# Stick breaking: a part of the products of sigmoid and running product moved from VectorE to GpSimd

## The chip, the cores and the metric

The kernel runs on one core of a Trainium2 chip. The core has five engines that matter here: PE (TensorE), VectorE (DVE in the profile), ScalarE (ACT), GpSimd (POOL) and SyncE (SP), which issues the transfers. Each executes its own list of instructions in order and waits on semaphores for the others. The metric is the device time of one execution in microseconds; lower is better. Times before are three runs: 3091.64, 3101.06 and 3104.94 us, median 3101.06 us.

## The reference

Two encoder layers over 2064 tokens (16 meta tokens and 2048 others) of width 1024. The first has eight stick-breaking heads beside eight latent-attention heads (MLA), the second eight sliding-window heads (SWA) beside eight forgetting heads (FoX). The change touches only the stick breaking:

```python
z = jnp.einsum('bqhd,bkhd->bhqk', q[:, q0:q1], k[:, :q1]).astype(jnp.float32) * scale
past = jnp.arange(q1)[None, :] < jnp.arange(q0, q1)[:, None]
log_stay = jnp.where(past, jax.nn.log_sigmoid(-z), 0.0)
log_after = lax.cumsum(log_stay, axis=3, reverse=True) - log_stay
w = jnp.where(past, jnp.exp(jax.nn.log_sigmoid(z) + log_after), 0.0)
outs.append(jnp.einsum('bhqk,bkhd->bqhd', w.astype(v.dtype), v[:, :q1]))
```

The weight of a key is sigmoid(z) of that key, times the product of sigmoid(-z) over the keys between it and the query.

## The kernel before

The tokens are held in reverse order, so that the keys between a key and the query stand ahead of it in a row, and the sum over logarithms becomes a running product from left to right. A tile is 128 queries; its keys go in chunks of at most 512 columns (the last one with the 16 meta keys). For each pair of heads and each chunk, PE puts the scores of both heads into two PSUM banks (line 1087). For each head `sb_sig` then emits five steps:

1. ScalarE: sigmoid(-z) from the bank into columns 1 to n of `b` (`sig1`, line 1407). `b` and `pc` are the two halves of one row buffer of 1026 fp32; there are four such buffers (`sbr`).
2. VectorE: a scan forms the running product of `b` into `pc` (`scan`, line 1415 for the first chunk, 1417 for the others, which start from the last column of the chunk before).
3. ScalarE: sigmoid(z) in place in the PSUM bank (`sig2`, line 1410). It needs the scan for nothing.
4. VectorE: `pc` = bank times `pc` (line 1431), when both are there (`signed`). After it `mulled` gives the bank back and announces the chunk.
5. `pv_hi`: ScalarE casts `pc` to fp16 (line 1205, for meta keys 1207), then VectorE or GpSimd subtracts to form the low half (line 1218, for meta keys 1220). Then a DMA transposes both halves (line 588) and PE multiplies them with the values (lines 1278 to 1280).

While these go on, the same engines make the projections of the next heads: PE at lines 825 and 915, ScalarE and VectorE at lines 936, 937, 970, 972, 1770 and 1771, and the preparation of weights at lines 653, 655, 698 and 755 (VectorE, ScalarE, GpSimd).

The order on every engine comes from a planner, `Flow`, when the program is built. It keeps a clock of its own, a queue of jobs for each engine by priority, and for each engine a sum of the costs that stand in its queue or run, `f.load`. Costs are formulas, as `dve(n)` = 1.042 n + 69 ns and `gps(n)` = 1.88 n + 150 ns. A job is emitted when the planner's clock has its engine free. Of the subtraction of step 5 the planner decides where it goes by these loads, when the cast is done:

```python
onD = f.load["D"] + d + LOBIAS < f.load["G"] + g      # line 1213, LOBIAS = 1000 ns
```

So a job that is moved or costed otherwise changes the order of everything that follows, on all engines.

Of the kernel before, what the change touches and what calls it, by code (L numbers as in the profile page):

```python
# [15 lines left out]
AF = mybir.ActivationFunctionType  # L16
ALU = mybir.AluOpType
# [3 lines left out]
D = 1024  # L21
# [379 lines left out]
def act(n, ap=False, sb=False):  # L401
    return 0.834 * n + 50.0 + (93.0 if ap else 0.0) + (42.0 if sb else 0.0)


def dve(n):
    return 1.042 * n + 69.0


def gps(n):
    return 1.88 * n + 150.0  # L410
# [15 lines left out]
class Kern:  # L426
# [974 lines left out]
    def sb_sig(self, ps, n, e, i, prev, read, v):  # L1401
        nc, f, it = self.nc, self.f, e.it
        r, pr = it.r, it.pr
        b, pc = v[:, 0:513], v[:, 513:1026]

        def sig1():
            nc.scalar.activation(b[:r, 1:n + 1], ps[:r, :n], AF.Sigmoid, scale=pr.scn[:r])  # L1407

        def sig2():
            nc.scalar.activation(ps[:r, :n], ps[:r, :n], AF.Sigmoid, scale=pr.scp[:r])  # L1410

        def scan():
            if i == 0:

                nc.vector.tensor_tensor_scan(pc[:r, :n + 1], b[:r, :n + 1], self.diag[:r, :n + 1], 0.0, ALU.mult, ALU.add)
            else:
                nc.vector.tensor_tensor_scan(pc[:r, :n + 1], b[:r, :n + 1], self.diag[:r, :n + 1], prev[0], ALU.mult, ALU.bypass)  # L1417
            prev[0] = pc[:r, n:n + 1]

        both = [2]  # L1420

        def scanned():

            if i:
                read(i - 1)
            signed()

        def signed():
            both[0] -= 1
            if not both[0]:  # L1430
                f.job("D", dve(n), lambda: nc.vector.tensor_tensor(pc[:r, :n], ps[:r, :n], pc[:r, :n], ALU.mult), mulled, e.pr)  # L1431

        def mulled():
            self.bk.free("S", ps)
            e.done = lambda: read(i)
            self.pv_ready(e, pc)

        f.job("A", act(n, True), sig1, lambda: f.job("D", 2.08 * n + 135.0, scan, scanned, e.pr), e.pr)
        f.job("A", act(n, True), sig2, signed, e.pr)


    def sm_item(self, pr, u, mask, done, stored):
# [2022 lines left out]
```

## Time and profile before

| | |
|---|---|
| median of three runs | 3101.06 us |
| the profiled execution | 3114.27 us |
| its span in the trace | 3112.2 us |
| busy: PE, VectorE, ScalarE, GpSimd | 84%, 78%, 57%, 51% |
| stick breaking | about 100 to 1000 us |
| mean granted clock of PE | 0.94 of full speed |

An engine's busy time is the time in which it had an instruction running, and an instruction that waits inside itself, for a port for example, counts as busy. Idle time stands beside the next instruction, with what ended it. The stages of the kernel overlap: while stick breaking runs, PE already makes projections for what follows.

### The profile page before, as it was taken

The page shows a single profiled execution, that of the slowest core. Times are in us where ns is not written, and L with a number is a line of the kernel's source. Part 1 is how long each engine was busy: PE and PEld are TensorE (multiplying, and loading weights), DVE is VectorE, ACT ScalarE, POOL GpSimd, SP SyncE. Part 2 cuts the span into 40 slices and gives each one's busy share as a digit, 9 for nine tenths or more (in the row PEclk, how much of TensorE's full clock was granted, in tenths as well). Part 3 has the DMA queues.
Part 4 walks back from the last instruction along what each step waited for, and adds up shares of the span by engine and source line. Part 5 has one row for each costly group of instructions (what it writes and reads, how often), then busy time and mean ns, then how long its engine had stood idle before and what let it go on. Part 6 is the DMA issues. An engine that isn't in the chain of part 4 may idle for free. (4 is left out here: it accounts for less than half of the span.)

```text
span 3112.2 us, 88537 instructions
## 1 busy us (share of the span) xinstructions
PE 2608.2 (84%) x34261; PEld 1794.9 (58%) x34261; DVE 2439.8 (78%) x6874; ACT 1775.4 (57%) x4082; POOL 1576.6 (51%) x2292
## 2 busy tenths in 40 slices
PE   4888988888887798888776799968969797799998
PEld 2676766766775455545554355646746465566643
DVE  8889899989998786667686875866757576588866
ACT  4667677757875465556575335455465554566611
POOL 3566566755754354445465534344454443456500
PEclk9989999999998999999887899989989899899999
DMA  4365465666798699999999985777667666555863
GB/s 153 54 125 108 98 120 113 114 115 108 128 162 186 166 196 215 221 212 188 164 166 168 215 205 87 145 134 141 115 125 134 118 128 107 101 123 100 177 166 112
DMA packets 1206808, 444.62 MB, mean 143 GB/s; under 512 B 1091616, under 2 KB 1171584, under 8 KB 1206384
## 3 DMA queue, kind: packets, MB, share of 16 engines
q1 hardware_dynamic: 1204048, 430.50, 71.1%
q0 software_dynamic: 2336, 8.46, 0.8%
q8 instruction: 268, 4.39, 0.6%
q14 instruction: 156, 1.28, 0.1%
HBM read 119.62 MB, written 51.06 MB: 55 GB/s over the span
## 5 line engine op out<-in xcount | busy, mean ns | idle before, releaser
L1218 POOL TENSOR_TENSOR mem<-mem 128x512 f16<-128x512 f32 (+3 forms) x751 | 823.6, 1107 | 440.4 <-ACT mem L1205 414.1
L825 PE MATMUL bank<-mem 128*128 128x512 f16 (+2 forms) x4272 | 929.1, 369 | 8.7 <-DVE mem L1485 2.6
L1205 ACT CAST mem<-mem 128x512 f16<-128x512 f32 (+3 forms) x1080 | 520.3, 513 | 276.6 <-DMA mem<-mem 134.4
L825 PEld LDWEIGHTS <-mem 128*128 128x128 f16 (+1 forms) x4272 | 405.9, 100 | 438.6 <-issue 88.2
L1278 PE MATMUL psO<-mem 128*128 128x64 f16 x3264 | 403.8, 200 | 294.4 <-DMA mem<-mem 287.8
L915 PE MATMUL bank<-mem 128*128 128x128 f16 x9984 | 643.7, 221 | 5.5 <-DVE mem L970 4.1
L915 PEld LDWEIGHTS <-mem 128*128 128x128 f16 x9984 | 578.3, 99 | 49.4 <-issue 41.0
L1087 PE MATMUL bank<-mem 64*128 64x256 f16 (+8 forms) x6264 | 521.3, 286 | 47.4 <-DVE mem L1431 22.5
L1278 PEld LDWEIGHTS <-mem 128*128 128x128 f16 x3264 | 307.4, 101 | 426.9 <-DMA mem<-mem 367.0
L1522 ACT ACTIVATE mem<-mem,smt,p 128x656 f32<-128x656 f32 (+16 forms) x264 | 336.3, 1275 | 237.3 <-DVE smt L1519 206.7
L1280 PE MATMUL psO<-mem 128*128 128x64 f16 x3264 | 400.6, 199 | 0.0
L1279 PE MATMUL psO<-mem 128*128 128x64 f16 x3264 | 400.5, 199 | 0.0
L1087 PEld LDWEIGHTS <-mem 64*128 64x128 f16 (+1 forms) x6264 | 271.8, 96 | 195.8 <-issue 100.1
L1279 PEld LDWEIGHTS <-mem 128*128 128x128 f16 x3264 | 310.3, 102 | 15.2 <-issue 2.4
L1280 PEld LDWEIGHTS <-mem 128*128 128x128 f16 x3264 | 311.1, 102 | 0.0
L1218 DVE TENSOR_TENSOR mem<-mem 128x512 f16<-128x512 f32 (+3 forms) x329 | 254.8, 791 | 66.4 <-ACT mem L1205 62.9
L1417 DVE TENSOR_TENSOR_SCAN mem<-mem 128x513 f32<-128x513 f32 (+2 forms) x224 | 290.7, 1325 | 4.9 <-ACT mem L1407 4.6
L1550 POOL TENSOR_TENSOR ist<-ist,p 128x2 f32<-128x2 f32 (+1 forms) x196 | 49.7, 254 | 425.1 <-DVE ist L1547 406.1
L1490 DVE CUSTOM_DVE_ANT_0 mem<-bank,mem 128x256 f32<-128x256 f32 (+6 forms) x484 | 195.5, 455 | 74.2 <-PE bank L1093 48.9
L1407 ACT ACTIVATE mem<-bank,p 128x512 f32<-128x512 f32 (+3 forms) x360 | 213.1, 592 | 45.0 <-PE bank L1087 44.4
L1325 POOL TENSOR_TENSOR mem<-mem 128x128 f16<-128x128 f32 (+1 forms) x264 | 136.9, 522 | 176.1 <-ACT mem L1322 174.3
L1485 DVE TENSOR_SCALAR_CACHE_REDUCE mem<-bank 128x512 f32<-128x512 f32 (+5 forms) x372 | 188.8, 545 | 38.3 <-PE bank L1093 22.6
(191 smaller groups left out, 4130.2 us busy)
## 6 DMA issues: line engine op xcount, KB each, us to landing
mem<-in_w_dram SPq DMA_DIRECT2D x46, 512.0 KB, 4.0
tmp_mx_dram<-mem SPq DMA_DIRECT2D x128, 128.0 KB, 2.4
mem<-in_wout_dram SPq DMA_DIRECT2D x32, 512.0 KB, 4.3
mem<-mem SPq DMA_TRANSPOSE x988, 3.4
mem<-tmp_cqT_dram SPq DMA_DIRECT2D x12, 1024.0 KB, 6.5
mem<-in_xr_dram SPq DMA_DIRECT2D x16, 512.0 KB, 4.5
tmp_res_dram<-mem POOLq DMA_DIRECT2D x16, 512.0 KB, 5.0
mem<-tmp_res_dram SPq DMA_DIRECT2D x16, 512.0 KB, 5.3
```

Source lines behind the costliest of these rows:

```text
L825: nc.tensor.matmul(out, lhsT=st(kt, a), rhs=mv(kt, b), start=i == 0 and j == 0, stop=i == m - 1 and j == 2)
L915: nc.tensor.matmul(ps[:, 128 * i:128 * i + 128], lhsT=mv(a)[:, kt, 128 * i:128 * i + 128], rhs=w[b][:, kt, c0:c0 + 128], start=i == 0 and ...
L1087: nc.tensor.matmul(o, lhsT=l, rhs=m, start=i == 0, stop=mask is None and i == len(run) - 1)
L1205: nc.scalar.copy(t[:r, a:a + w], e.P[:r, e.pcol:e.pcol + w])
L1218: eng.tensor_tensor(t[:r, a + w:a + 2 * w], e.P[:r, e.pcol:e.pcol + w], t[:r, a:a + w], ALU.subtract)
L1278: nc.tensor.matmul(out, lhsT=p[:, a, :r], rhs=vt[:, hd, 0, :], start=e.first and i == 0 and hd == 0, stop=False)
L1279: nc.tensor.matmul(out, lhsT=p[:, a, :r], rhs=vt[:, hd, 1, :], start=False, stop=False)
L1280: nc.tensor.matmul(out, lhsT=p[:, b, :r], rhs=vt[:, hd, 0, :], start=False, stop=False)
L1407: nc.scalar.activation(b[:r, 1:n + 1], ps[:r, :n], AF.Sigmoid, scale=pr.scn[:r])
L1417: nc.vector.tensor_tensor_scan(pc[:r, :n + 1], b[:r, :n + 1], self.diag[:r, :n + 1], prev[0], ALU.mult, ALU.bypass)
L1490: nc.vector.tensor_tensor_reduce(row[:r, o + oo:o + oo + w], ps[:r, oo:oo + w], pr.cum[kb][hd][:r, ko:ko + w], 1.0, -3e38, ALU.add, ALU.ma ...
L1522: nc.scalar.activation(row[:r, :n], row[:r, :n], AF.Exp, bias=st[:r, 1:2], scale=sc[:r], accum_out=it.st[:r, hd:hd + 1])
```

## The change

When `sb_sig` is called for a chunk of a head, it compares two loads of the planner: `onG` holds if GpSimd's load with the new multiplication (1.15 times `gps(n)`) is less than VectorE's load. If it doesn't hold, the five steps are as before. If it holds:

- step 3 is emitted only after the scan (`sig3`, line 1428 of the changed kernel), and writes sigmoid(z) into columns 1 to n of `b`, in place of the sigmoid(-z) that the scan has read. At its end the PSUM bank is given back;
- step 4 is on GpSimd (`weigh`, line 1425): `pc` = `b` times `pc`, all in on-chip memory;
- step 5 follows as before.

```diff
         both = [2]
+        d, g = dve(n), 1.15 * gps(n)
+        onG = f.load["G"] + g < f.load["D"]
+
+        def weigh():
+            nc.gpsimd.tensor_tensor(pc[:r, :n], b[:r, 1:n + 1], pc[:r, :n], ALU.mult)
+
+        def sig3():
+            nc.scalar.activation(b[:r, 1:n + 1], ps[:r, :n], AF.Sigmoid, scale=pr.scp[:r])
 
         def scanned():
 
             if i:
                 read(i - 1)
-            signed()
+            if onG:
+                f.job("A", act(n, True), sig3, lambda: [self.bk.free("S", ps), f.job("G", g, weigh, mulled, e.pr)], e.pr)
+            else:
+                signed()
...
         def mulled():
-            self.bk.free("S", ps)
+            if not onG:
+                self.bk.free("S", ps)
             e.done = lambda: read(i)
             self.pv_ready(e, pc)
 
         f.job("A", act(n, True), sig1, lambda: f.job("D", 2.08 * n + 135.0, scan, scanned, e.pr), e.pr)
-        f.job("A", act(n, True), sig2, signed, e.pr)
+        if not onG:
+            f.job("A", act(n, True), sig2, signed, e.pr)
```

Lines behind the change move: the multiplication that stays on VectorE is line 1442 of the changed kernel, and all lines from 1442 of before on stand 13 lower.

How this looks in the lists of instructions, at its first place, two scans of 273 columns early in the stick breaking. VectorE, the difference (- before, + changed); `mem` is on-chip memory, `bank` a PSUM bank, `p` a column of scale factors:

```order
 L1417 SCALAR_TENSOR_TENSOR mem<-mem 128x273 x2
-L1431 TENSOR_TENSOR mem<-bank_85,mem 128x272
-L1431 TENSOR_TENSOR mem<-bank_84,mem 128x272
 L98 TENSOR_SCALAR p2t<-p_24_376 128x1
 L110 TENSOR_SCALAR p_32_801<-p2t 128x1
```

The two multiplications behind the scans are gone from VectorE; the next work follows the scans at once.

ScalarE at the same place, the difference:

```order
 L1407 ACTIVATE mem<-bank_85,p_24_376 128x272
-L1410 ACTIVATE bank_85<-bank_85,p_24_376 128x272
 L1407 ACTIVATE mem<-bank_84,p_24_376 128x272
-L1205 CAST mem<-mem 128x256
-L1410 ACTIVATE bank_84<-bank_84,p_24_376 128x272
-L1205 CAST mem<-mem 128x256
+L1205 CAST mem<-mem 128x256 x2
+L1407 ACTIVATE mem<-bank_83,p_24_376 128x512
+L1428 ACTIVATE mem<-bank_85,p_24_376 128x272
+L1428 ACTIVATE mem<-bank_84,p_24_376 128x272
```

The second sigmoid no longer follows the first of its bank; both stand behind two casts and the first sigmoid of the next chunk, and write on-chip memory instead of the bank.

GpSimd at the same place, before:

```order
L790 TENSOR_TENSOR nr<-amr,half 128x1 x3
L1218 TENSOR_TENSOR mem<-mem 128x256 x3
L1220 TENSOR_TENSOR mem<-mem 128x2x16
L1218 TENSOR_TENSOR mem<-mem 128x256
L1220 TENSOR_TENSOR mem<-mem 128x2x16
L1218 TENSOR_TENSOR mem<-mem 128x512 x2
```

and in the changed kernel:

```order
L790 TENSOR_TENSOR nr<-amr,half 128x1 x3
L1218 TENSOR_TENSOR mem<-mem 128x256 x2
L1425 TENSOR_TENSOR mem<-mem 128x272 x2
L1218 TENSOR_TENSOR mem<-mem 128x256
L1220 TENSOR_TENSOR mem<-mem 128x2x16
L1218 TENSOR_TENSOR mem<-mem 128x256
L1220 TENSOR_TENSOR mem<-mem 128x2x16
L1218 TENSOR_TENSOR mem<-mem 128x512 x2
```

The two multiplications stand ahead of the subtractions of their own chunk, and all that follows on GpSimd stands behind them. Counted over the whole lists: 119 multiplications are on GpSimd and 241 stay on VectorE; 26 subtractions of line 1218 and 9 of line 1220 go from GpSimd to VectorE.

## Rows read from the trace of the kernel before

**Rows 1.** Page, heading and busy time of the engines over the span.
```profile
span 3112.2 us, 88537 instructions
PE 2608.2 (84%) x34261; PEld 1794.9 (58%) x34261; DVE 2439.8 (78%) x6874; ACT 1775.4 (57%) x4082; POOL 1576.6 (51%) x2292
```
**Rows 2.** Busy us, 100 to 1000: PE, PEld, DVE, ACT, POOL; clock, DMA, GB/s.
```profile
100.00:1000.00 900.00, 769.34 (x11737) 596.30 (x11736) 841.82 (x1405) 641.69 (x1467) 569.60 (x571) 0.97 0.65 121
```
**Rows 3.** Line 1417: count, duration min/median/max in ns, first and last start.
```profile
L1417 DVE TENSOR_TENSOR_SCAN mem<-mem x224: 487/1274/2460, 118.6 to 990.5; 128x513 f32<-128x513 f32 x48, 128x273 f32<-128x273 f32 x28, 128x145 f32<-128x145 f32 x12, 128x401 f32<-128x401 f32 x12
```
**Rows 4.** Waits, 100 to 1000 us, by engine: waiter, releaser, us, times, longest.
```profile
DVE mem L1364 <- PE psO L1282: 10.0, 13, 1.9
DVE mem L1417 <- ACT mem L1407: 4.6, 4, 1.6
...
ACT mem L1205 <- DVE mem L1431: 54.7, 53, 3.4
...
POOL mem L1218 <- ACT mem L1205: 229.3, 140, 4.9
...
PE psO L1278 <- DMA mem<-mem: 72.6, 74, 4.2
```
**Rows 5.** Timeline of VectorE and GpSimd, 439 to 456 us: start, us, what.
```profile
439.39 1.21 DVE L1415 TENSOR_TENSOR_SCAN mem<-mem 128x513 f32<-128x513 f32 x1
439.65 1.66 POOL L1218 TENSOR_TENSOR mem<-mem 128x384 f16<-128x384 f32 x1 [3.09 <-ACT mem L1205]
441.47 0.92 POOL L1218 TENSOR_TENSOR mem<-mem 128x384 f16<-128x384 f32 x1
...
447.05 1.28 DVE L1417 TENSOR_TENSOR_SCAN mem<-mem 128x513 f32<-128x513 f32 x1 [1.58 <-ACT mem L1407]
...
450.83 1.16 POOL L1218 TENSOR_TENSOR mem<-mem 128x512 f16<-128x512 f32 x1 [4.58 <-ACT mem L1205]
451.19 0.67 DVE L1431 TENSOR_TENSOR mem<-bank,mem 128x512 f32<-128x512 f32 x1
...
452.47 0.75 DVE L1417 TENSOR_TENSOR_SCAN mem<-mem 128x257 f32<-128x257 f32 x1
...
454.14 2.87 POOL L755 TENSOR_TENSOR mem<-mem 128x1024 bf16<-128x1024 f16 x1
455.18 2.38 DVE L1417 TENSOR_TENSOR_SCAN mem<-mem 128x257 f32<-128x257 f32 x1
```
**Rows 6.** Instructions by line and shape, 100 to 1000 us: busy us, mean ns, idle.
```profile
L1417 DVE TENSOR_TENSOR_SCAN mem<-mem 128x513 f32<-128x513 f32 x96 | 157.9, 1667 | 3.6 <-ACT mem L1407 3.3
L1431 DVE TENSOR_TENSOR mem<-bank,mem 128x512 f32<-128x512 f32 x192 | 123.8, 674 | 0.8
L1431 DVE TENSOR_TENSOR mem<-bank,mem 128x144 f32<-128x144 f32 x32 | 8.3, 290 | 0.0
L1218 DVE TENSOR_TENSOR mem<-mem 128x512 f16<-128x512 f32 x6 | 4.8, 796 | 0.0
L1407 ACT ACTIVATE mem<-bank,p 128x512 f32<-128x512 f32 x192 | 132.8, 691 | 28.0 <-PE bank L1087 27.6
L1218 POOL TENSOR_TENSOR mem<-mem 128x512 f16<-128x512 f32 x186 | 273.3, 1483 | 158.6 <-ACT mem L1205 140.9 <-issue 12.9 <-DMA mem<-in_ropeq_dram 3.3
L1218 POOL TENSOR_TENSOR mem<-mem 128x256 f16<-128x256 f32 x87 | 81.6, 943 | 61.9 <-ACT mem L1205 61.9
L1218 POOL TENSOR_TENSOR mem<-mem 128x128 f16<-128x128 f32 x25 | 18.6, 745 | 13.8 <-ACT mem L1205 9.0 <-DVE mem L1431 4.7
```
**Rows 7.** The same stretch by line, all shapes together.
```profile
L1417 DVE TENSOR_TENSOR_SCAN mem<-mem 128x513 f32<-128x513 f32 (+2 forms) x224 | 290.7, 1325 | 4.9 <-ACT mem L1407 4.6
L1415 DVE TENSOR_TENSOR_SCAN mem<-mem 128x513 f32<-128x513 f32 (+5 forms) x134 | 154.2, 1166 | 2.7 <-ACT mem L1407 1.5 <-POOL mem L1218 1.0
L1220 DVE TENSOR_TENSOR mem<-mem 128x32 f16<-128x32 f32 (+1 forms) x18 | 4.0, 222 | 0.0
```
**Rows 8.** Line 2279, fp32 on GpSimd behind the stage: ns min/median/max.
```profile
L2279 POOL TENSOR_TENSOR mem<-mem x8: 1262/1286/1464, 1045.3 to 1460.2; 128x512 f32<-128x512 f32 x6, 128x528 f32<-128x528 f32 x2
```

## The prediction, made before the changed kernel ran

> **What bounds the kernel now.** I read the page's busy times first, then the busy time of the stage that the change touches, then each engine's waits inside it. Over the whole run no engine is full: PE 84%, VectorE 78%, GpSimd 51% [rows 1]. In the stage it is different. Scans of stick breaking start from 118.6 to 990.5 us [rows 3], so the stage is 100 to 1000 us, and there VectorE is busy for 841.8 of 900 us (94%), PE for 769.3 (85%), ScalarE for 641.7 (71%), GpSimd for 569.6 (63%) [rows 2]. VectorE's idle 58 us come in scraps: the wait that costs it most sums to 10.0 us. The others wait for longer: GpSimd 229.3 us for the casts of line 1205, ScalarE 54.7 us for the very multiplication that is moved, PE 72.6 us for transposes [rows 4]. So VectorE sets the pace, and a microsecond taken from it here is worth about one at the end, until PE is full; PE would allow 900 - 769 = 131 us, more than any figure below. Outside the stage hardly anything changes engines.
>
> But VectorE's busy time is not all work. A 513-wide scan takes 1.28 us at 447.05 [rows 5], and the mean of the 96 from line 1417 is 1667 ns [rows 6]. A 257-wide one takes 0.75 us at 452.47, and 2.38 us at 455.18, where a GpSimd instruction runs from 454.14 to 457.01. It goes the other way too: a 384-wide subtraction on GpSimd takes 0.92 us at 441.47, and 1.66 us at 439.65, where a scan had started 0.26 us before [rows 5]. Whichever starts later waits for the other. The multiplication that is moved reads one operand from PSUM and shows nothing of this: 0.67 us at 451.19, inside a subtraction on GpSimd [rows 5], and 674 ns in the mean [rows 6].
>
> **The change part by part.** The order of the changed kernel has 119 of 360 multiplications on GpSimd: 42 of 512 columns, 12 of 400, 26 of 272, 18 of 256, 17 of 144 and 4 tiny ones.
>
> *Taken from VectorE.* 674 ns for 512 columns, 290 for 144 [rows 6], and on the line between these 557, 424 and 407 for 400, 272 and 256: 42 x 674 + 12 x 557 + 26 x 424 + 18 x 407 + 17 x 290 ns = 28.3 + 6.7 + 11.0 + 7.3 + 4.9 = 58 us.
>
> *Given back to VectorE.* As GpSimd's load rises in the planner's account, more subtractions of line 1218 go to VectorE: in this stage 25 more, 14 of them of 512 columns, with 9 small ones of line 1220. At 796 ns for all 25 (the 512-wide mean [rows 6]) and 222 for the small ones [rows 7] that is 19.9 + 2.0 = 22 us. A saving of 36 us is left.
>
> *ScalarE.* As many sigmoids as before. The second one now writes on-chip memory, as the first does (691 ns for 512 columns [rows 6]). What changes is its place: it waits for the scan, and behind it in ScalarE's queue stand casts and the next first sigmoids. VectorE has the other head's scan meanwhile, which covers it, so I count nothing; without that cover VectorE would stand idle for up to the sigmoid's 0.69 us (rival three). The PSUM bank is given back at the end of the second sigmoid instead of the multiplication, each some 0.7 us after the scan: nothing.
>
> *GpSimd.* The trace of before has no such multiplication. The nearest rows are an fp32 sum of 512 columns behind the stage, 1286 ns median [rows 8], and in the stage the subtractions of line 1218, with the waiting in them: 1483 ns for 512 columns, 943 for 256, 745 for 128 [rows 6]. I take the latter, and 1213 midway between the first two for 400: 42 x 1483 + 12 x 1213 + 44 x 943 + 17 x 745 = 62.3 + 14.6 + 41.5 + 12.7 = 131 us. Off go 14 subtractions of 512, 4 of 384 (1213), 6 of 256, 1 of 128 and at most 745 ns for each of 9 small ones: 20.8 + 4.9 + 5.7 + 0.7 + 6.7 = 39 us. So GpSimd goes from 570 to 662 us of 900, 74%. It has the time, so these 92 us are not on the path by themselves. Behind a multiplication in GpSimd's queue stand subtractions, hence the transposes that PE waits for [rows 4].
>
> *The new collisions* are the disputed term. Today the 224 scans of line 1417 have 374 columns in the mean and take 1325 ns; undisturbed they would take 0.99 (estimated on the line through 0.75 and 1.28 us [rows 5]). The 134 of line 1415 have 433 and take 1166 ns [rows 7], against 1.04 on a line of the same slope through 1.21 us for 513. The waiting is 224 x 0.335 + 134 x 0.126 = 75 + 17 = 92 us. Lower bound: it grows with GpSimd's busy time, 92/570 = 0.16 us for each; 92 us more give 15 us. Upper bound: every multiplication makes a scan wait for its whole undisturbed length, 119 x 340 columns x 1286/512 ns, that is 119 x 0.85 = 101 us. Between them: the multiplications were the part of VectorE's work under which GpSimd could run freely, and this shrinks just where GpSimd gets more to do; that speaks for more than 15. Against the upper end: much of the waiting falls on GpSimd, where it costs nothing (186 subtractions of 512 columns at 1483 ns, 1.16 us undisturbed [rows 5, 6], are 60 us). I take 30 us, twice the lower bound and nearer to it, since the mean scan waits only 92/358 = 0.26 us now.
>
> Sum: -58 + 22 + 30 = -6 us. The profiled execution took 3114.27 us, 2 more than its span of 3112.2 [rows 1], and lies 13 us above the median of 3101.06; a difference of this size carries over, so the forecast is 3095 us: no change that can be measured, since about 0.5% (15.5 us) is what a measurement of this kernel can tell from none.
>
> The Trainium skill, "SBUF — State Buffer", section "Who interferes with whom", calls what VectorE and GpSimd share there an exclusive lock, taken by a VectorE instruction with two SBUF inputs against a GpSimd one that reads SBUF. The trace agrees (0.92 against 1.66 us). By this rule the change trades work that is free of the lock for work that takes it, which is the second rival.
>
> **The rivals.** *One, the saving stays.* Collisions grow by the lower bound or not at all: -36 + 15 = -21 us, or -36 us: 3065 to 3080 us. For it: the planner moves a multiplication only where it sees GpSimd with less to do, and GpSimd is idle for 330 us. Against it: GpSimd is idle because it waits for casts that follow the scans, so it becomes ready when VectorE is at the next scan. Chance 0.34.
>
> *Two, slower: the collisions eat more than the saving.* A multiplication on GpSimd is 0.85 us in which no scan can begin, or it waits for a scan and then delays the next. From 36 + 15.5 = 51.5 us of new waiting, 0.43 us for each of 119, the kernel is slower by more than 0.5%; at the upper bound it is 101 - 36 = +65 us. At 0.6 us each, the middle, it is 71 - 36 = +35 us: 3136 us. For it: scans of 2.38 instead of 0.75 us occur. Against it: the mean of 0.26 us. Chance 0.20.
>
> *Three, the longer way:* scan, sigmoid, GpSimd, cast. If VectorE stands idle for the sigmoid at half of the 119, 0.5 x 119 x 0.69 = +41 us come on top of -6: 3136 us. Against it: VectorE's scans of line 1417 wait for the first sigmoid for only 4.6 us in all [rows 4]. Chance 0.06.
>
> That the planner moves nothing is excluded by the order.
>
> **How the numbers follow.** No change 0.40, with 3086 to 3116 us as its own range; faster (rival one) 0.34; slower (two and three) 0.26. The likeliest is no change, 3095 us. The range that leaves out 2 in 10 goes from the far end of rival one, 3065, to the middle of rival two, 3136.
>
> **What would show it.** Right: VectorE's busy time in the stage falls by less than 20 us though its own multiplications fall by 58; the 513-wide scans of line 1417 rise from 1667 to some 1800 ns; GpSimd is at 70 to 77%; the last scan starts within 15 us of before. Rival one: the scans keep their mean, and the last one starts 20 us or more earlier. Rival two: 513-wide scans over 1900 ns, and VectorE still over 93% busy in a longer stage. Rival three: VectorE idle for well over 58 us, with waits ended by line 1407. A shift of over 15 us that arises behind the stage would be outside all of these.

## The result and the profile after

The changed kernel takes 3129.91 us in the median of four runs (3125.24 to 3130.98), against 3102.18 for the kernel before. The ratio on record is 1.0079, with an interval of [1.0057, 1.0101]; the two medians alone stand 27.7 us apart. It is **slower**, by some 24 us if one goes by the ratio, as the table below does throughout. The forecast was no change at 3095 us: the range held the time, the sign did not.

PE's mean granted clock was 0.932 to 0.938 of full speed in these four runs; in the one at 0.938 the changed kernel took 3125.24 us, where the kernel before at 0.938 took 3096.13 to 3112.46 us in the runs beside the experiments, so the clock doesn't account for the difference.

The profiled executions stand 16.7 us apart (3114.27 and 3130.98 us), less than the 24 of the ratio; that of before lies above its timed runs. Heading of the changed kernel's page and busy time of the engines over the span, against [rows 1]:

```profile
span 3129.2 us, 88405 instructions
PE 2623.1 (84%) x34261; PEld 1804.8 (58%) x34261; DVE 2436.7 (78%) x6793; ACT 1777.7 (57%) x4082; POOL 1667.8 (53%) x2373
```

VectorE has 3 us less to do than before, GpSimd 91 us more, and the kernel is longer. The stage from 100 to 1000 us, with the columns of [rows 2] (PE, PEld, VectorE, ScalarE, GpSimd, clock, DMA share, GB/s):

```profile
100.00:1000.00 900.00, 762.64 (x11623) 591.42 (x11620) 834.21 (x1309) 641.00 (x1455) 660.67 (x651) 0.96 0.62 117
```

GpSimd goes from 569.6 to 660.7 us (73%; 662 was forecast). VectorE falls by 7.6 us, and PE by 6.7, since less of its work fits into the stretch. Line 1417 of the changed kernel, against [rows 3]: the last scan starts 6.2 us later.

```profile
L1417 DVE TENSOR_TENSOR_SCAN mem<-mem x224: 483/1270/2846, 119.6 to 996.7; 128x513 f32<-128x513 f32 x48, 128x273 f32<-128x273 f32 x28, 128x145 f32<-128x145 f32 x12, 128x401 f32<-128x401 f32 x12
```

The same stretch by line, all shapes together (busy us, mean ns, idle before it and what ended it), against [rows 7]; L1442 is the multiplication left on VectorE, L1425 the one on GpSimd, L1428 its sigmoid:

```profile
L1417 DVE TENSOR_TENSOR_SCAN mem<-mem 128x513 f32<-128x513 f32 (+2 forms) x224 | 294.4, 1336 | 1.9 <-ACT mem L1407 1.6
L1415 DVE TENSOR_TENSOR_SCAN mem<-mem 128x513 f32<-128x513 f32 (+5 forms) x136 | 158.4, 1182 | 6.6 <-ACT mem L1407 3.9 <-issue 1.2 <-POOL mem L1218 1.1
L1442 DVE TENSOR_TENSOR mem<-bank,mem 128x512 f32<-128x512 f32 (+5 forms) x241 | 135.5, 578 | 4.2 <-ACT bank L1410 0.2
L1425 POOL TENSOR_TENSOR mem<-mem 128x512 f32<-128x512 f32 (+5 forms) x119 | 133.6, 1131 | 41.3 <-ACT mem L1428 40.7
L1218 DVE TENSOR_TENSOR mem<-mem 128x512 f16<-128x512 f32 (+3 forms) x49 | 45.3, 925 | 9.0 <-ACT mem L1205 8.7
L1220 DVE TENSOR_TENSOR mem<-mem 128x32 f16<-128x32 f32 x26 | 10.5, 405 | 0.0
```

By shape, against [rows 6]:

```profile
L1218 POOL TENSOR_TENSOR mem<-mem 128x512 f16<-128x512 f32 x172 | 257.2, 1506 | 100.4 <-ACT mem L1205 99.0 <-POOL mem L1218 0.7 <-POOL mem L1325 0.3
L1417 DVE TENSOR_TENSOR_SCAN mem<-mem 128x513 f32<-128x513 f32 x96 | 154.8, 1630 | 0.2
L1425 POOL TENSOR_TENSOR mem<-mem 128x512 f32<-128x512 f32 x42 | 61.3, 1466 | 18.6 <-ACT mem L1428 18.6
L1218 DVE TENSOR_TENSOR mem<-mem 128x512 f16<-128x512 f32 x20 | 23.1, 1153 | 2.3 <-ACT mem L1205 2.1
```

The scans did not get longer (513 columns: 1667 before, 1630 now), so the sign most looked for is absent. What got longer on VectorE is the subtraction: 796 ns before, 1153 now. The waits of the stage, against [rows 4] (waiter, releaser, us in total, times, longest):

```profile
DVE mem L1364 <- PE psO L1282: 13.6, 13, 2.7
...
DVE mem L1417 <- ACT mem L1407: 1.6, 2, 1.0
...
ACT mem L1205 <- DVE mem L1442: 62.0, 68, 3.4
ACT mem L1428 <- DVE mem L1417: 58.0, 59, 3.3
ACT mem L1205 <- POOL mem L1425: 30.2, 39, 2.4
...
POOL mem L1218 <- ACT mem L1205: 146.8, 110, 5.3
POOL mem L1425 <- ACT mem L1428: 40.7, 33, 3.8
...
PE psO L1278 <- DMA mem<-mem: 82.0, 76, 3.5
```

Two waits are new on ScalarE: 58.0 us of the second sigmoid for the scan, and 30.2 us of the cast for GpSimd's product. All its waits together are hardly more (257 us against 252 before, summed over the view), so ScalarE is not short of time; if its new waits cost anything, it is through what stands behind them in its list. GpSimd's wait for casts has fallen from 229.3 to 146.8 us: more often it is still at something else when its input is there. Of the 119 products only 33 found it waiting for their sigmoid. One place, in the timeline from 299 to 306 us (start, us, engine, what; in brackets the wait ahead):

```profile
299.01 3.32 DVE L1417 TENSOR_TENSOR_SCAN mem<-mem 128x513 f32<-128x513 f32 x2
299.23 4.06 POOL L1218 TENSOR_TENSOR mem<-mem 128x512 f16<-128x512 f32 x2 [4.11 <-ACT mem L1205]
300.32 0.69 ACT L1428 ACTIVATE mem<-bank,p 128x512 f32<-128x512 f32 x1 [0.53 <-DVE mem L1417]
...
303.25 1.27 POOL L1425 TENSOR_TENSOR mem<-mem 128x512 f32<-128x512 f32 x1
...
304.55 1.14 ACT L1205 CAST mem<-mem 128x512 f16<-128x512 f32 x2 [0.79 <-POOL mem L1425]
```

The sigmoid ends at 301.01. The product starts 2.24 us later, because two subtractions, which themselves shared the stretch with two scans, fill GpSimd from 299.23 on. It takes 1.27 us (VectorE's took 0.67 [rows 6]), and ScalarE stands 0.79 us at the cast.

### The profile page after: what moved, and what is told of

The parts are those of the page before. It is cut to its first block, busy times and chain, and to the rows that moved or that the text cites. A ratio compares the mean times of both kernels' runs of the same rounds, so it can differ in the third digit from the quotient of the medians.

```text
span 3129.2 us, 88405 instructions
## 1 busy us (share of the span) xinstructions
PE 2623.1 (84%) x34261; PEld 1804.8 (58%) x34261; DVE 2436.7 (78%) x6793; ACT 1777.7 (57%) x4082; POOL 1667.8 (53%) x2373
## 3 DMA queue, kind: packets, MB, share of 16 engines
q14 instruction: 155, 1.27, 0.1%
## 5 line engine op out<-in xcount | busy, mean ns | idle before, releaser
L1218 POOL TENSOR_TENSOR mem<-mem 128x512 f16<-128x512 f32 (+3 forms) x725 | 787.3, 1096 | 331.1 <-ACT mem L1205 327.5
L1218 DVE TENSOR_TENSOR mem<-mem 128x256 f16<-128x256 f32 (+3 forms) x355 | 281.1, 808 | 66.8 <-ACT mem L1205 64.8
L1417 DVE TENSOR_TENSOR_SCAN mem<-mem 128x513 f32<-128x513 f32 (+2 forms) x224 | 294.4, 1336 | 1.9 <-ACT mem L1407 1.6
L1407 ACT ACTIVATE mem<-bank,p 128x512 f32<-128x512 f32 (+3 forms) x360 | 210.4, 592 | 30.4 <-PE bank L1087 30.2
```

The costliest lines, as they stand in the source:

```text
L1218: eng.tensor_tensor(t[:r, a + w:a + 2 * w], e.P[:r, e.pcol:e.pcol + w], t[:r, a:a + w], ALU.subtract)
```

## The experiments

All shifts below are the ratio less one, times 3105 us; the interval of each ratio makes a shift uncertain by 3 to 8 us. **Left over** is what the change of VectorE's busy time doesn't explain: the shift less 0.66 times the difference of VectorE's busy time over the whole span to the 2439.8 us of [rows 1]. The 0.66 is an estimate from one run, f1_psum_before, which takes 75.0 us from VectorE in the order of before and is 49.4 us faster; that run also makes GpSimd's instructions shorter, so it is not VectorE's relief alone. e2_on_dve against e1_light gives 0.72 in another order. The runs that change only the order leave 4 and 5 us, and e6_late and f3_psum_late -4 and -6, so less than about 6 means nothing. "Cast's wait" is the wait of line 1205 for the product where that is on GpSimd, from 100 to 1000 us.

Not every run fell where its expectation wanted it. e8_memset (3105.45 us) and g2_lat30 (3121.58) lie between the two ranges given for them, e9_lokeep (3124.23) likewise, e4_many (3175.53) lies above both, f2_psum_after (some 12 us behind f1 where 15 were asked) and g3_psum_lat15 (7 us where 10 or under 5 were) fit neither side cleanly.

| kernel | ratio to before | shift, us | VectorE busy, whole span | cast's wait, us | left over, us |
|---|---|---|---|---|---|
| after | 1.0079 [1.0057, 1.0101] | +24.5 | 2436.7 | 30.2 | 27 |
| e1_light | 0.9926 [0.9901, 0.9950] | -23.0 | 2393.1 | 9.3 | 8 |
| e8_memset | 1.0000 [0.9985, 1.0015] | 0.0 | 2396.8 | 39.6 | 28 |
| e2_on_dve | 1.0072 [1.0050, 1.0094] | +22.4 | 2456.2 | | 12 |
| e3_order_b | 0.9992 [0.9979, 1.0005] | -2.5 | 2429.8 | | 4 |
| e3_order_c | 0.9997 [0.9983, 1.0011] | -0.9 | 2430.8 | | 5 |
| e4_few (55 products) | 1.0008 [0.9998, 1.0019] | +2.5 | 2440.5 | 4.0 | 2 |
| e4_many (174 products) | 1.0229 [1.0205, 1.0253] | +71.1 | 2420.9 | 127.3 | 84 |
| e6_late | 0.9968 [0.9952, 0.9983] | -9.9 | 2430.6 | | -4 |
| e9_lokeep | 1.0067 [1.0049, 1.0085] | +20.8 | 2442.9 | 41.9 | 19 |
| f1_psum_before | 0.9841 [0.9819, 0.9863] | -49.4 | 2364.8 | | 0 |
| f2_psum_after | 0.9880 [0.9854, 0.9905] | -37.3 | 2352.3 | 30.8 | 20 |
| f3_psum_late | 0.9829 [0.9809, 0.9848] | -53.1 | 2368.7 | | -6 |
| g1_lat15 | 1.0050 [1.0032, 1.0068] | +15.5 | 2443.7 | 3.6 | 13 |
| g2_lat30 | 1.0047 [1.0029, 1.0064] | +14.6 | 2438.1 | 4.0 | 16 |
| g3_psum_lat15 | 0.9860 [0.9839, 0.9881] | -43.5 | 2359.4 | 5.8 | 10 |

### The product's cost at an unchanged order: e1_light, e8_memset, e2_on_dve

All three have the list of instructions of the changed kernel; only what stands where the product stood is different.

```diff
         def weigh():
-            nc.gpsimd.tensor_tensor(pc[:r, :n], b[:r, 1:n + 1], pc[:r, :n], ALU.mult)
+            nc.gpsimd.tensor_tensor(pc[:r, :1], b[:r, 1:2], pc[:r, :1], ALU.mult)
```

> The changed kernel with every instruction at its place, but the 119 multiplications on GpSimd take one column instead of 144 to 512, so the products of the other columns are left out. It takes away GpSimd's added work and what collides with it, and keeps the new order and the late second sigmoid. Collisions as the cause: VectorE keeps its 58 us of relief and GpSimd gets its 113 us back, so it is at least 30 us faster than the changed kernel, 3070 to 3100 us, with the last scan some 25 us earlier. The late sigmoid as the cause (ScalarE waits 60 us for scans): within 10 us of the changed kernel, 3120 to 3140 us. The new order alone as the cause: the stage shortens, but the later stages keep their delay of some 10 us.

In e8_memset two fills of the whole width stand before the one column:

```diff
         def weigh():
-            nc.gpsimd.tensor_tensor(pc[:r, :n], b[:r, 1:n + 1], pc[:r, :n], ALU.mult)
+            nc.gpsimd.memset(b[:r, 1:n + 1], 0.0)
+            nc.gpsimd.memset(b[:r, 1:n + 1], 0.0)
+            nc.gpsimd.tensor_tensor(pc[:r, :1], b[:r, 1:2], pc[:r, :1], ALU.mult)
```

> The changed kernel with every instruction at its place. In place of each multiplication on GpSimd stand two fills of the same width, which read nothing, and one column of the product; the rest of the products is left out. GpSimd is busy for about as long as with the multiplications (some 1.3 us for 512 columns) but reads nothing meanwhile. Collisions as the cause: within 12 us of the run with one column, 3070 to 3095 us. GpSimd's time itself as the cause (what is queued behind it comes later): near the changed kernel, 3115 to 3135 us.

And e2_on_dve has the product on VectorE, with both operands in on-chip memory:

```diff
         def weigh():
-            nc.gpsimd.tensor_tensor(pc[:r, :n], b[:r, 1:n + 1], pc[:r, :n], ALU.mult)
+            nc.vector.tensor_tensor(pc[:r, :n], b[:r, 1:n + 1], pc[:r, :n], ALU.mult)
```

> The changed kernel with every instruction at its place in the program, but the 119 multiplications are given to VectorE, both operands in on-chip memory. If VectorE sets the pace one to one, as I predicted with, it gets 55 to 60 us of work back, less some 20 us of collisions that go: 3155 to 3175 us. If the port that both share sets the pace, GpSimd's work of 113 us leaves it and 58 us come to it: within 10 us of the changed kernel or faster, 3110 to 3140 us. If the new order or the late sigmoid costs the time: the first figure as well, since that order is kept.

These three settle most. With one column the kernel is 0.74% faster than before, with fills of the product's length as fast, with the product 0.79% slower. By line, e1_light, 100 to 1000 us:

```profile
L1417 DVE TENSOR_TENSOR_SCAN mem<-mem 128x513 f32<-128x513 f32 (+2 forms) x224 | 275.4, 1251 | 3.4 <-ACT mem L1407 2.4 <-POOL mem L1220 0.8
L1425 POOL TENSOR_TENSOR mem<-mem 128x1 f32<-128x1 f32 (+1 forms) x119 | 46.3, 393 | 57.7 <-ACT mem L1428 57.2
```

The same of e8_memset, where the fills are lines 1425 and 1426 and the column is 1427, with its multiplication on VectorE at line 1444:

```profile
L1417 DVE TENSOR_TENSOR_SCAN mem<-mem 128x513 f32<-128x513 f32 (+2 forms) x224 | 270.9, 1230 | 8.8 <-ACT mem L1407 5.9 <-POOL mem L1220 1.5 <-POOL mem L1427 0.7
L1426 POOL MEMSET mem<- 128x512 f32 (+5 forms) x119 | 45.6, 383 | 6.8
L1425 POOL MEMSET mem<- 128x512 f32 (+5 forms) x119 | 45.5, 382 | 38.2 <-ACT mem L1430 37.8
L1427 POOL TENSOR_TENSOR mem<-mem 128x1 f32<-128x1 f32 (+1 forms) x119 | 44.8, 377 | 9.5
```

Busy time over the span, then the stretch from the first scan's start to the last one's end (length, then PE, PEld, VectorE, ScalarE, GpSimd as above), then ScalarE's wait at the cast; first e1_light:

```profile
PE 2606.4 (84%) x34261; PEld 1799.4 (58%) x34261; DVE 2393.1 (77%) x6793; ACT 1773.0 (57%) x4082; POOL 1570.7 (51%) x2373
97.70:960.70 863.00, 748.60 (x11573) 585.76 (x11574) 790.08 (x1302) 635.75 (x1453) 566.54 (x649) 0.97 0.66 121
ACT mem L1205 <- POOL mem L1425: 9.3, 14, 2.0
```

and e8_memset:

```profile
PE 2610.9 (84%) x34261; PEld 1796.4 (58%) x34261; DVE 2396.8 (77%) x6793; ACT 1776.7 (57%) x4082; POOL 1643.8 (53%) x2611
98.50:976.20 877.70, 756.67 (x11588) 587.70 (x11589) 790.22 (x1302) 638.68 (x1453) 638.78 (x887) 0.96 0.65 119
ACT mem L1205 <- POOL mem L1427: 39.6, 49, 2.4
```

*First step, one column to fills: +23 us* (uncertain by some 9, the two intervals taken together). GpSimd is busy for 45.6 + 45.5 + 44.8 = 136 us at this place, against 134 for the products, but VectorE is not kept busier: 2396.8 against 2393.1 us, and its scans of line 1417 take 1230 against 1251 ns. So these 23 us come from GpSimd's time and not from collisions with VectorE. VectorE stands idle instead: of the stretch of its scans, it is idle for 72.9 us in e1_light and 87.5 in e8_memset, 14.6 more. ScalarE's wait at the cast goes from 9.3 to 39.6 us (that for VectorE's products falls from 45.7 to 35.2). What the fills don't do is read. The Trainium skill, "SBUF — State Buffer", section "Who interferes with whom", says that a VectorE instruction with two SBUF inputs contends with a GpSimd one that reads SBUF and not with one that only writes it; the equal scans agree.

*Second step, fills to product: +24.5 us.* VectorE's busy time rises from 2396.8 to 2436.7 us, its scans of line 1417 from 1230 to 1336 ns. The lists are the same but for the product, so these are the collisions of the product's reads: 40 us, 0.34 us for each of 119 products.

e2_on_dve is as slow as the changed kernel: with both operands in on-chip memory and in lists planned for GpSimd, the product costs as much on VectorE as on GpSimd. It adds 63 us to VectorE's busy time over e1_light and 45 us to the time. If VectorE's time counted one to one, it should have taken 3155 us or more; it took 3128.61.

What is left over is not GpSimd's product alone. e1_light leaves 8 us with one column and e2_on_dve 12 with nothing of the product on GpSimd. What these two share with the changed kernel, its lists and the late sigmoid, can account for that much, and the runs don't separate it; the 23 us between e1_light and e8_memset don't hold it.

### The order alone: e3_order_b, e3_order_c

The kernel before, with the planner's cost of a scan a few ns lower or (139.0) higher, so that everything is emitted in another order:

```diff
-        f.job("A", act(n, True), sig1, lambda: f.job("D", 2.08 * n + 135.0, scan, scanned, e.pr), e.pr)
+        f.job("A", act(n, True), sig1, lambda: f.job("D", 2.08 * n + 131.0, scan, scanned, e.pr), e.pr)
```

> The kernel before, with the planner's cost of a scan at 131 instead of 135 ns beside its share by column. Nothing is moved between steps; only the order of the lists differs. If the order alone is worth 10 us or more either way: outside 3090 to 3115 us. If collisions or the late sigmoid are the cause: within 3092 to 3112 us, as before.

> The same with 139 ns. Order alone: outside 3090 to 3115 us, and another time than with 131 ns. Collisions or the late sigmoid: within 3092 to 3112 us.

Both agree with before within 0.1%, so a lucky order of before is not the cause. That the changed kernel's order is not an unlucky one is not shown by these two; e9_lokeep, g1_lat15 and g2_lat30 speak against it, which order the lists otherwise with 104 to 111 products moved and are all 0.5 to 0.7% slower than before. Line 1417 of e3_order_b:

```profile
L1417 DVE TENSOR_TENSOR_SCAN mem<-mem x224: 486/1272/2865, 119.6 to 970.9; 128x513 f32<-128x513 f32 x48, 128x273 f32<-128x273 f32 x28, 128x145 f32<-128x145 f32 x12, 128x401 f32<-128x401 f32 x12
```

Its last scan starts 19.6 us earlier than before's (990.5 [rows 3]), and nothing is gained: from the first scan's start to the last one's end VectorE is busy for 20.7 us less than in before (817.3 against 838.0), so other work was only put behind the scans. The start of the last scan is therefore a poor gauge between kernels of different order, and the prediction had chosen it.

### How many products: e4_few, e4_many

The changed kernel, with GpSimd's cost overstated (55 products moved) or (`0.5 * gps(n)`) understated (174 moved):

```diff
-        d, g = dve(n), 1.15 * gps(n)
+        d, g = dve(n), 2.5 * gps(n)
```

> The changed kernel with 2.5 instead of 1.15 times GpSimd's cost in the test, so 55 multiplications move instead of 119. If each moved multiplication costs more than it saves (some 25 us for 119): 3106 to 3122 us. If the first ones, where GpSimd has least to do, are a gain and only the later ones cost: 3085 to 3100 us.

> The same with 0.5: 174 move. If each costs: 3133 to 3155 us. If the loss came from a few unlucky places: about as the changed kernel, 3120 to 3133 us.

55 products cost nothing that can be measured, 119 cost 24.5 us, 174 cost 71. The loss grows faster than the number, and not with VectorE's busy time, which is 19 us below before's in e4_many. What grows is ScalarE's wait at the cast for GpSimd, 4.0, 30.2 and, in e4_many:

```profile
ACT mem L1205 <- POOL mem L1425: 127.3, 113, 5.1
```

In that kernel's stage VectorE's idle time is 126.5 us, against 54.5 before (first scan's start to last scan's end).

### The late sigmoid: e6_late

In the changed kernel the sigmoid stays behind the scan, but in the PSUM bank, and the product goes to VectorE (148 times):

```diff
         def weigh():
-            nc.gpsimd.tensor_tensor(pc[:r, :n], b[:r, 1:n + 1], pc[:r, :n], ALU.mult)
+            nc.vector.tensor_tensor(pc[:r, :n], ps[:r, :n], pc[:r, :n], ALU.mult)
 
         def sig3():
-            nc.scalar.activation(b[:r, 1:n + 1], ps[:r, :n], AF.Sigmoid, scale=pr.scp[:r])
+            nc.scalar.activation(ps[:r, :n], ps[:r, :n], AF.Sigmoid, scale=pr.scp[:r])
...
-                f.job("A", act(n, True), sig3, lambda: [self.bk.free("S", ps), f.job("G", g, weigh, mulled, e.pr)], e.pr)
+                f.job("A", act(n, True), sig3, lambda: f.job("D", d, weigh, mulled, e.pr), e.pr)
...
-            if not onG:
-                self.bk.free("S", ps)
+            self.bk.free("S", ps)
```

> The late second sigmoid alone: where the test holds (148 times here) the second sigmoid comes after the scan, but it stays in the PSUM bank and the multiplication stays on VectorE. Late sigmoid as the cause: 3120 us or more. Collisions as the cause: within 12 us of before, 3095 to 3118 us.

It is 0.3% faster than before. The sigmoid behind the scan costs nothing where the lists are planned with the product on VectorE, so the longer way hurts through GpSimd's part of it.

### The scans without the collision: f1_psum_before, f2_psum_after, f3_psum_late

A scan of line 1417 has a second operand that its second operation (bypass) ignores. It lies in on-chip memory; here a column of the chunk's PSUM bank stands for it. f1 is the kernel before with this one line, f2 the changed kernel, f3 the kernel of e6_late.

```diff
-                nc.vector.tensor_tensor_scan(pc[:r, :n + 1], b[:r, :n + 1], self.diag[:r, :n + 1], prev[0], ALU.mult, ALU.bypass)
+                nc.vector.tensor_tensor_scan(pc[:r, :n + 1], b[:r, :n + 1], ps[:r, 0:1].to_broadcast([r, n + 1]), prev[0], ALU.mult, ALU.bypass)
```

> The kernel before, every instruction at its place. The 224 scans of line 1417 ignore their second operand; here it is read from the chunk's PSUM bank instead of on-chip memory, so that a scan has one operand in on-chip memory like the multiplication that doesn't collide. Collisions as what fills VectorE's time: the 513-wide mean falls from 1667 to about 1290 ns, and GpSimd's 512-wide subtractions from 1483 to under 1350; some 75 us leave VectorE and the kernel is 40 to 75 us faster, 3030 to 3065 us. If what stands in the durations is not waiting for GpSimd, the mean stays above 1550 ns and the time within 15 us of before, 3092 to 3122 us.

> The same edit in the changed kernel. Collisions as the cause of the slowdown: most of the waiting that the moved multiplications make is gone, VectorE keeps at least part of its 58 us, and this is faster than the kernel before with the same edit, by 5 to 25 us. If the late sigmoid or the traffic through GpSimd is the cause: slower than that by 15 us or more, as the change is without the edit.

> A candidate: scans with their ignored operand from PSUM, multiplications all on VectorE, and the late second sigmoid where the test holds. If the gains of the two runs add (1.6% and 0.3%): 3040 to 3052 us. If the late sigmoid adds nothing: 3052 to 3062 us.

f1 is 1.6% faster than before. By line and by shape, f1, 100 to 1000 us:

```profile
L1417 DVE TENSOR_TENSOR_SCAN mem<-mem,bank 128x513 f32<-128x513 f32 (+2 forms) x224 | 214.4, 979 | 16.0 <-ACT bank L1410 11.1 <-POOL mem L1218 2.0 <-issue 0.9
...
L1218 POOL TENSOR_TENSOR mem<-mem 128x512 f16<-128x512 f32 x186 | 223.6, 1216 | 176.4 <-ACT mem L1205 161.7 <-issue 8.7 <-DMA mem<-in_ropeq_dram 4.2
L1417 DVE TENSOR_TENSOR_SCAN mem<-mem,bank 128x513 f32<-128x513 f32 x96 | 120.3, 1270 | 12.9 <-ACT bank L1410 8.8 <-POOL mem L1218 1.5 <-issue 0.9
```

The 513-wide scan falls from 1667 to 1270 ns, and GpSimd's subtraction from 1483 to 1216 [rows 6]: nearly all the waiting of both is gone at once (undisturbed, they take 1.28 and 1.16 us [rows 5]). This confirms how the prediction read [rows 5]. Its estimate of the waiting in the scans of line 1417 was 75 us; they fall from 290.7 [rows 7] to 214.4 us, by 76.

With the scans freed, moving the product still loses: f2 is at 0.9880 and f1 at 0.9841, though VectorE has 12.5 us less to do in f2. The two intervals touch, but the fastest of f2's six runs (3060.68 us) is slower than the slowest of f1's five (3059.91). VectorE is idle for 95.1 us from the first scan's start to the last one's end, against 70.6 in f1. That fits the time of GpSimd again, seen where collisions with the scans of line 1417 can't be its cause: 20 us left over, in which the 8 to 12 us of the order may be contained.

f3 has the lowest ratio (3051.64 us median); its interval covers f1, so the two are not told apart. Both beat the kernel before and the changed one.

### Fewer subtractions given back: e9_lokeep

The subtractions' rule no longer counts the products that wait for GpSimd (`self.wl` is the sum of their costs, added when one is queued and taken off when it is done):

```diff
-            onD = f.load["D"] + d + LOBIAS < f.load["G"] + g
+            onD = f.load["D"] + d + LOBIAS < f.load["G"] - self.wl + g
```

> The changed kernel, but the planner leaves the waiting multiplications out of GpSimd's load when it decides where a subtraction goes, so fewer subtractions go to VectorE (345 instead of 355 in the whole list). If the subtractions given back to VectorE, 34 us instead of the 22 I counted, are what makes the loss: 3108 to 3122 us. If GpSimd's own time and reads make it: 3125 to 3140 us, since GpSimd has more to do.

Only 10 fewer subtractions went to VectorE. 1.0067 lies within the interval of the changed kernel; on what giving back costs, the run is inconclusive.

### ScalarE's wait at the cast: g1_lat15, g2_lat30, g3_psum_lat15

The planner takes the product for ready 1.5 us (g2: 3000.0, 3 us) after its cost says so, and so puts the cast later in ScalarE's list; g3 is f2 with the same 1.5 us.

```diff
-                f.job("A", act(n, True), sig3, lambda: [self.bk.free("S", ps), f.job("G", g, weigh, mulled, e.pr)], e.pr)
+                f.job("A", act(n, True), sig3, lambda: [self.bk.free("S", ps), f.job("G", g, weigh, mulled, e.pr, 1500.0)], e.pr)
```

> The changed kernel, but the planner takes each product of GpSimd for ready 1.5 us later than its cost says, so that ScalarE's cast of it and VectorE's follow-up stand later in their lists (104 products on GpSimd instead of 119). If ScalarE's wait in list order for the product is what the lateness costs, its wait at the cast for GpSimd falls from 30 us of the stage to under 10 and the time comes down by 10 to 20 us, to 3108 to 3120. If the lateness acts elsewhere (the products merely come late for the product matrices), that wait falls or stays and the time is 3125 to 3135; the 15 fewer products by themselves explain about 4 us of a fall.

> The same with 3 us (107 products on GpSimd). By the first theory the wait at the cast falls further and the time stays near that of the run with 1.5 us, 3105 to 3120; by the second the products come later still for what needs them and the time is 3125 to 3140.

> The changed kernel with the 1.5 us and with the scans' ignored operand in PSUM, so that reads of GpSimd hardly collide with the scans. By the first theory it lies 10 us or more below the 3070.6 of the same kernel without the 1.5 us, at 3050 to 3060; by the second within 5 us of it, and the 15 fewer products by themselves explain about 2 us.

Waits of ScalarE in g1_lat15, 100 to 1000 us:

```profile
ACT mem L1205 <- DVE mem L1442: 70.3, 64, 3.5
ACT mem L1428 <- DVE mem L1417: 55.9, 55, 3.0
ACT mem L1407 <- PE bank L1087: 37.8, 36, 2.9
...
ACT mem L1205 <- POOL mem L1425: 3.6, 7, 0.9
```

The wait at the cast falls from 30.2 to 3.6 us, as the first theory wanted (that ScalarE's wait in list order is the cost). The time comes down by less than it wanted: 1.0050, at the upper edge of the 3108 to 3120 that it gave (3120.58, beside a before of 3107.02), and the intervals of g1 and of the changed kernel overlap. Other waits of ScalarE grew instead: 62.0 to 70.3 us for VectorE's product, 28.7 to 37.8 for the scores. g2 is like g1. g3 lies some 6 us under f2, between the two theories, and their intervals overlap too. What is left over falls from 27 to 13 and 16 us, and from 20 to 10. Of the first two falls some 4 to 5 us belong to the 15 and 12 products that are no longer moved (from e4_few to the changed kernel 64 more products cost 22 us). So ScalarE's place in line is at most some half of the loss that isn't VectorE's. The 10 to 16 us that stay are no more than e1_light and e2_on_dve leave without the product on GpSimd, within the noise, so that a late product makes them is not shown. The second theory, that the products come late for the product matrices, has no support either: PE's wait for the transposes (line 1278) falls from 82.0 us in the changed kernel to 55.5 in g1 and 63.9 in g2. Through which wait GpSimd's lateness reaches the end is not settled.

## Why the prediction was wrong

**The sum for VectorE came out right, from terms that did not; that is luck.** Forecast: -58 + 22 + 30 = -6 us. Measured: -7.6 in the stretch of [rows 2], -3.1 over the span.
- *Taken away:* 58 us forecast, 51 measured (186.7 us for 359 multiplications before, by line, 135.5 for 241 now).
- *Given back:* 22 forecast. Lines 1218 and 1220 on VectorE take 45.3 + 10.5 = 55.8 us; before it was 4.0 for line 1220 [rows 7] and 17.9 for 24 of line 1218. That is 34 us. The number was right (25 and 8 more), the price was not: 796 ns came from 6 instructions of the kernel before; it is 1153 ns for 20 now. Only a part of that is the product's doing: in e1_light, where the products are one column, the same 20 take 964 ns already.
- *Collisions:* 30 forecast. From fills to product VectorE's busy time rises by 40 us, inside the bounds of 15 and 101, and partly in the subtractions just named. Against the kernel before, the scans of both lines show only 8 us (452.8 against 444.9); without the product's reads they would have become shorter (275.4 + 148.5 = 423.9 us in e1_light).

**ScalarE** was right for the sigmoid: e6_late has it late 148 times, in the bank, and loses nothing.

**GpSimd's busy time** was right (662 forecast, 660.7 measured), and what was concluded from it is **the step that failed**: "It has the time, so these 92 us are not on the path by themselves." e8_memset against e1_light puts 23 us on exactly this, at equal VectorE time; f2 against f1 agrees, with up to 20 us that the collisions of line 1417 can't make. An engine at 73% has the time, but not at the moment at which it is wanted. The product is the middle of a chain of scan, sigmoid, product and cast, it stands behind subtractions (4 us of them at the place shown), and the cast holds up ScalarE's list. The prediction had the warning in its own rows. It named the subtractions and transposes *behind* a product in GpSimd's queue, and priced neither these nor the cast that waits for the product. How much of the 23 us goes which way stays open: the wait at the cast can be all but removed (g1_lat15) and most of the loss stays.

**The worth of a microsecond** was the second error. "A microsecond taken from it here is worth about one at the end" is refuted: e1_light takes 46.7 us from VectorE and gains 23, f1_psum_before takes 75.0 and gains 49. At 94% busy VectorE is the main bound of the stage but not the only one; a third to a half of what it was spared in these two runs was lost to idle time. With 0.66 the forecast's -6 becomes -4, and GpSimd's lateness, some 20 to 27 us, decides the sign.

**The rivals.** Rival one (the saving stays) fell: there was almost none. Rival two had its sign and half of its mechanism: the collisions of the product's reads cost some 24 us (fills to product), but its test, 513-wide scans over 1900 ns, failed at 1630. Rival three came nearest: VectorE's idle time in the stage rose from 54.5 to 64.7 us, but its waits are not ended by line 1407 (1.6 us), and the sigmoid is not what costs: GpSimd's step is. Neither rival alone gives the result: it is a saving of VectorE's that is eaten by collisions and by what is given back, and a lateness of GpSimd's on top.

**Behind the stage** the prediction expected nothing. In the profiles the last scan starts 6.2 us later and the end comes 16.7 later. PE's multiplications of line 2094 belong to the next stage and are begun in this one. In the kernel before:

```profile
L2094 PE MATMUL bank<-mem x1632: 216/219/314, 815.7 to 1027.6; 128*128 128x128 f16 x171, 128*16 128x128 f16 x11
```

In the changed kernel they are line 2107:

```profile
L2107 PE MATMUL bank<-mem x1632: 216/219/314, 845.0 to 1036.9; 128*128 128x128 f16 x171, 128*16 128x128 f16 x11
```

The last of them starts 9.3 us later, and the first step of the latent attention (line 1485, now 1498) starts at 1066.5 instead of 1053.8 us, 12.7 later. Part of the loss thus shows only behind the stage. That PE's later multiplications pass it on is argued from these times and was not tested, and how the remaining 4 us arise was not followed.

**What would have made it right:** pricing a moved link of a chain by the time from its input being ready to its output being ready (2.24 + 1.27 us at the place shown, where VectorE takes 0.67 for the work itself), not by its engine's share of busy time.

## What to carry to other kernels

An idle share is no offer to take a link of a dependent chain: look at what stands in that engine's queue when the link's input becomes ready, and at which engine waits for it in list order. Convert busy time saved on the busiest engine into time by an experiment that takes it away as nearly alone as can be (here 0.5 to 0.7 us came out for each), before it is set against other terms. Where two engines collide at on-chip memory, look first for an operand that can lie elsewhere: one ignored operand moved to PSUM gave 1.6%, while moving work between the colliding engines gave a loss.

## What the hardware showed beyond what was expected

The scan waits for GpSimd on account of an operand that it ignores: with the operand in PSUM (f1_psum_before) the longest of the 224 scans of line 1417 takes 1284 ns, against 2460 before [rows 3]. In f1:

```profile
L1417 DVE TENSOR_TENSOR_SCAN mem<-mem,bank x224: 482/1024/1284, 118.5 to 931.7; 128x513 f32<-128x513 f32 x48, 128x273 f32<-128x273 f32 x28, 128x145 f32<-128x145 f32 x12, 128x401 f32<-128x401 f32 x12
```

Not every instruction that got longer did so through the moved products. Line 626, a bf16 operation with a scalar, takes 491 ns in the changed kernel and 318 before (the same 19 instructions), but as long in e3_order_c, where nothing is moved to GpSimd and only the order differs. The changed kernel and e3_order_c, 100 to 1000 us:

```profile
L626 DVE TENSOR_SCALAR amd<-idbf,wmm 128x128 bf16<-128x128 bf16 x19 | 9.3, 491 | 0.0
L626 DVE TENSOR_SCALAR amd<-idbf,wmm 128x128 bf16<-128x128 bf16 x19 | 9.6, 503 | 0.0
```

What makes it long no run here shows. One mean against one mean of another order can't be laid to the change.
